# Seven Strassen pairs in place of five in each output projection, with part of the rests on GpSimd

## The chip, the cores and the metric

The kernel runs on one core of a Trainium2 chip. The metric is the time of one execution on the device in microseconds (us); of several runs the median counts. The engines are TensorE (PE; PEld is its weight load), VectorE (DVE), ScalarE (ACT), GpSimd (POOL) and SyncE (SP), whose queue issues the loads and stores here.

## The reference

One layer of an encoder on 512 tokens of width 1024, in fp32: a feed-forward block (FFN), a mixer (short convolution beside a two-way mLSTM), and a second FFN. Each block has a norm ahead and a norm behind it. Cut to the FFN, which the change concerns:

```python
def swiglu(x, w_in, w_out):
    gate, up = jnp.split(x @ w_in, 2, axis=-1)
    return (jax.nn.silu(gate) * up) @ w_out

def reference(...):
    h = swiglu(rmsnorm(x, norm_ffn1_pre), w_ffn1_in, w_ffn1_out)
    x = x + 0.5 * rmsnorm(h, norm_ffn1_post)
    ...   # the mixer, then the second FFN in the same form
```

x is 512x1024, w_in 1024x5632, w_out 2816x1024.

## The kernel before

**Splitting.** TensorE works on a 32-bit format of less precision (fp32r). So each fp32 operand is split: ScalarE casts it to a high part (L292), and a subtraction forms what is left of it, the rest or low part (L294, `split`). `split` takes the engine of that subtraction as its last argument; without one it is VectorE. A product of two operands is three matmuls: high x high, high x low, low x high. Only the first four weight tiles of the program (`ON_POOL`, L234) have their rests formed by GpSimd, with 1024 columns each.

**Input stage of an FFN** (`ffn`, L435). The 2816 columns of gate and up are 22 blocks of 128. The first two are multiplied plainly (L453). For each of the other 20, gate and up are one pair of tiles, and their product with the two halves of x is made by Strassen's scheme of seven products (L431, `mm_part`; 12 matmuls of 256 columns each, 84 a pair). `w_pair` (L151) prepares a pair's weights: four sums of 512 columns on VectorE (L158), then the splits of g, s1, g again and u: rests of 1024, 512, 1024 and 1024 columns, the last named `ul`. The results are joined by VectorE reading PSUM (L503, L505, L508, L484) and multiplied (L509). The fourth product of a pair comes after the first products of the next pair and adds to a bank that L508 has to have read.

**Output stage.** The 22 row blocks of w_out are taken in the order of the list `OUT` (L107). Five pairs of blocks (`SEVEN = 5`) are multiplied by the same scheme, the others plainly. A pair has a part a (products 1, 5, 6, 7) and a part b (2, 3, 4), and each product is six matmuls of 512 columns (L564), 42 a pair; a plain block "k" costs 24 (L589), two of them 48. First come parts a of all pairs; then each part b with a plain block behind it; then the last plain blocks. The last five (`TAIL`) are held back and multiplied token block by token block, each followed by its norm. `w_out_a` and `w_out_b` (L186, L209) form the sums of the weights (L191, L214) and split them; `left_a` and `left_b` (L540, L552) do the same with the activations (L531). After part a of the last pair `taken` moves banks to SBUF, because part b uses them again.

**Order.** TensorE's, VectorE's and the other engines' instructions are put in order by the tile scheduler, outside of a few pinned stretches at the start; each engine runs its instructions in that order. Weights come on SP's queue into four tiles of the pool `rawp`; the split weights live in 12 tiles of `wpool`. `mid` (L604) calls `wgates` (L696), which loads the mixer's gate weights and splits them on GpSimd; they are first used by the mixer's first products (L422).

Of the kernel before, what the change touches and what calls it, by code (L numbers as in the profile page):

```python
# [8 lines left out]
F32 = mybir.dt.float32  # L9
# [7 lines left out]
P = 128  # L17
# [3 lines left out]
KD = D // P  # L21
# [5 lines left out]
EPS = 1e-6  # L27
NEG = -1e30
TAIL = 5
SEVEN = 5  # L30
WARM = 20
WARM2 = 4
ON_POOL = (0, 1, 2, 3)
# [4 lines left out]
def encoder_kernel(ctx: ExitStack, tc: tile.TileContext, a: dict, out: bass.AP):  # L38
# [6 lines left out]
    rawp = ctx.enter_context(tc.tile_pool(name="rawp", bufs=4))  # L45
    gbp = ctx.enter_context(tc.tile_pool(name="gbp", bufs=2))
    t4p = ctx.enter_context(tc.tile_pool(name="t4p", bufs=2))
    t2p = ctx.enter_context(tc.tile_pool(name="t2p", bufs=6))
    small = ctx.enter_context(tc.tile_pool(name="small", bufs=4))
    psum = ctx.enter_context(tc.tile_pool(name="psum", bufs=8, space=PSUM))  # L50

# [54 lines left out]

    OUT = [("a", i) for i in range(SEVEN)]  # L107
    for i in range(SEVEN):
        OUT += [("b", i), ("k", 2 * SEVEN + i)]
    OUT += [("k", k) for k in range(3 * SEVEN, NF)]  # L110

    stream = []
    for w_in, w_out in ((w1i, w1o), (w2i, w2o)):
# [37 lines left out]
    def w_pair(g, u):  # L151


        def wt(n):
            return wpool.tile([P, 1024], F32R, tag="w", name=nm(n))

        def add(o, a_, b_, op):
            nc.vector.tensor_tensor(out=o, in0=a_, in1=b_, op=op)  # L158

        c = (slice(0, 512), slice(512, 1024))  # L160
        s1 = t2()
        add(s1, u[:, c[0]], u[:, c[1]], ALU.add)
        add(u[:, c[0]], g[:, c[0]], u[:, c[0]], ALU.subtract)
        gh, gl = wt("whi"), wt("wlo")
        split(gh, gl, g)
        add(g[:, c[0]], s1, g[:, c[0]], ALU.subtract)
        add(g[:, c[1]], g[:, c[1]], g[:, c[0]], ALU.subtract)
        s1w = wt("ws1")
        split(s1w[:, c[0]], s1w[:, c[1]], s1)
        ch_, cl = wt("whi"), wt("wlo")  # L170
        split(ch_, cl, g)
        uh, ul = wt("whi"), wt("wlo")
        split(uh, ul, u)

        def q(h_, l_, a_, b_):
            return tuple(v[:, r].rearrange("p (k f) -> p k f", k=KD // 2) for v, r in ((h_, a_), (l_, b_)))

        return {
            1: q(gh, gl, c[0], c[0]), 2: q(gh, gl, c[1], c[1]), 5: q(s1w, s1w, c[0], c[1]),
            6: q(ch_, cl, c[0], c[0]), 3: q(ch_, cl, c[1], c[1]),  # L180
            7: q(uh, ul, c[0], c[0]), 4: q(uh, ul, c[1], c[1]),
        }
# [3 lines left out]
    def w_out_a(r0, r1):  # L186

        c = (slice(0, 512), slice(512, 1024))

        def sub(o, a_, b_):  # L190
            nc.vector.tensor_tensor(out=o, in0=a_, in1=b_, op=ALU.subtract)  # L191

        def wt(n):
            return wpool.tile([P, 1024], F32R, tag="w", name=nm(n))

        sub(r1[:, c[0]], r0[:, c[1]], r0[:, c[0]])
        sub(r0[:, c[1]], r1[:, c[1]], r0[:, c[1]])
        t = t2()
        sub(t, r1[:, c[1]], r1[:, c[0]])
        kept.append(t)  # L200
        ah, al = wt("whi"), wt("wlo")
        split(ah, al, r0)
        bh, bl = wt("whi"), wt("wlo")
        split(bh[:, c[0]], bl[:, c[0]], r1[:, c[0]])
        split(bh[:, c[1]], bl[:, c[1]], t)
        return {1: (ah[:, c[0]], al[:, c[0]]), 7: (ah[:, c[1]], al[:, c[1]]),
                5: (bh[:, c[0]], bl[:, c[0]]), 6: (bh[:, c[1]], bl[:, c[1]])}

    def w_out_b(r1):  # L209

        c = (slice(0, 512), slice(512, 1024))
        hi, lo, t = (wpool.tile([P, 1024], F32R, tag="w", name=nm(n)) for n in ("whi", "wlo", "wt"))
        split(hi, lo, r1)
        nc.vector.tensor_tensor(out=r1[:, c[0]], in0=r1[:, c[0]], in1=kept.pop(0), op=ALU.subtract)  # L214
        split(t[:, c[0]], t[:, c[1]], r1[:, c[0]])
        return {2: (hi[:, c[0]], lo[:, c[0]]), 3: (hi[:, c[1]], lo[:, c[1]]), 4: (t[:, c[0]], t[:, c[1]])}

    def w_split(n):
# [57 lines left out]
    nc.gpsimd.memset(nhalf, -0.5)  # L276
    warm = const.tile([P, 256], BF16, name="warm")
    nc.gpsimd.memset(warm, 0.0)
    ones = const.tile([1, P], F32, name="ones")
    nc.gpsimd.memset(ones, 1.0)  # L280
    pw = ps()
    first = [ps() for _ in range(4)]
# [8 lines left out]
    def split(hi, lo, src, eng=nc.vector):  # L291
        latest["hi"] = nc.scalar.copy(out=hi, in_=src)  # L292
        pin(latest["hi"])
        latest["lo"] = eng.tensor_tensor(out=lo, in0=src, in1=f32(hi), op=ALU.subtract)  # L294
        pin(latest["lo"])
# [139 lines left out]
    def ffn(xq, between, finish, mid=None, within=None, ahead=(2, 2, 1, 1), late=None):  # L435
# [104 lines left out]
        def left_a(i):  # L540
            a_, b_ = hcol(2 * i), hcol(2 * i + 1)
            hi, lo = halves()
            s1 = t4()[:, 0:256]
            tt(s1, a_[:, early], b_[:, early], ALU.add)
            split(hi[:, 0:256], lo[:, 0:256], a_[:, later])
            tt(a_[:, early], a_[:, later], a_[:, early], ALU.subtract)
            tt(a_[:, later], s1, a_[:, later], ALU.subtract)
            split(hi[:, 256:512], lo[:, 256:512], s1)
            split(hi[:, 512:1024], lo[:, 512:1024], a_)
            return parts(hi, lo, {1: 0, 5: 256, 7: 512, 6: 768})  # L550

        def left_b(i):  # L552
# [42 lines left out]
        for at, (kind, n) in enumerate(OUT):  # L595
            if kind == "k":
# [4 lines left out]
                hT = (hs[:, q, 0:512], hs[:, q + 1, 0:512])  # L601
                split(hT[0], hT[1], hcol(n))
                ks[n] = (hT, w_get(min(2, len(OUT) - 1 - at)))
                if n == 12 and mid:  # L604
                    mid()
                if n < NF - TAIL:
                    for tb in range(NT):
# [86 lines left out]
    wg = {}  # L694

    def wgates():  # L696
        raw = small.tile([P, KD, 16], F32, tag="rawg", name="rawg", bufs=1)
        queued(raw, wm[:, GT:GT + 16].rearrange("(k p) f -> p k f", p=P))
        gt = bigt(F32R).rearrange("p q f -> p (q f)")
        nc.gpsimd.memset(f32(gt[:, 0:2048]), 0.0)  # L700
# [461 lines left out]
```

## Time and profile before

| | |
|---|---|
| median of 3 runs | 918.28 us (918.09 to 918.73) |
| the profiled execution | 915.36 us, its span 913.7 us |
| granted TensorE clock | 0.999 |
| busy: PE, PEld, DVE, ACT, POOL | 99%, 89%, 78%, 49%, 5% of the span |
| PE on the chain that ended last | 93% |
| first FFN: input stage, output stage | 36 to 228 us, 228 to about 345 us |
| second FFN: input stage, output stage | 594 to 799 us, 799 us to the end |

How to read it: the profile is of one execution, so sums are made against its own time. A row of a timeline gives the start and the length of an instruction, the engine, the line, the operation, what it writes and reads, shape and count, and in brackets how long the engine was idle ahead of it and for whom. A row of the groups gives busy time and mean length in ns, then idle time ahead and for whom. Tile names are the program's; `ps` is a PSUM bank, all other tiles are in SBUF.

### The profile page before, as it was taken

What the parts mean: (1) busy time and instruction counts of PE and PEld (TensorE: products, weight loads), DVE (VectorE), ACT (ScalarE), POOL (GpSimd) and SP (SyncE); (2) the same over time, 40 slices, a digit from 0 to 9 for tenths busy, and PEclk for the clock granted to TensorE, in tenths of its full rate; (3) what the DMA queues carried; (4) which work ended last, traced back from release to release, by engine and by line L of the source; (5) the groups of instructions that cost most, each with busy time, mean ns of one, the idle gap of its engine ahead of it and who ended that gap; (6) DMA issues with size and microseconds to landing.
All of it is one profiled execution on the core that took longest, in us unless ns stands there. A gap on an engine that the chain in (4) does not pass through costs nothing.

```text
span 913.7 us, 15022 instructions
## 1 busy us (share of the span) xinstructions
PE 900.1 (99%) x6015; PEld 816.7 (89%) x6015; DVE 716.2 (78%) x1196; ACT 444.6 (49%) x745; POOL 44.7 (5%) x67
## 2 busy tenths in 40 slices
PE   8999999999999999999999999999999999999997
PEld 7999999999877888987888888999999999977885
DVE  6988998888988359498787746889888988999435
ACT  6655555555456235452434335545545545566311
POOL 5000000000002001000011000000000000000000
PEclk9999999999999999999999999999999999999999
DMA  8233443343335614231422602224343432343402
GB/s 256 68 114 116 119 135 97 102 127 96 93 127 149 199 47 116 63 100 47 116 70 70 197 12 66 74 68 118 112 120 93 118 108 87 119 140 110 162 2 91
DMA packets 126257, 96.47 MB, mean 106 GB/s; under 512 B 4182, under 2 KB 114794, under 8 KB 126187
## 3 DMA queue, kind: packets, MB, share of 16 engines
q1 hardware_dynamic: 126186, 95.51, 35.1%
q8 instruction: 47, 0.77, 0.4%
q14 instruction: 24, 0.19, 0.1%
HBM read 93.40 MB, written 2.10 MB: 105 GB/s over the span
## 4 chain that ended last, share of the span: by engine, by line
PE 93%; DVE 4%; ACT 1%; issue 1%; DMA 1%; SPq 0%; POOL 0%; DVEq 0%; POOLq 0%; ACTq 0%
PE ps L431 43%; PE ps L589 13%; PE ps L422 12%; PE ps L564 9%; PE ps L453 5%; PE ps L1119 5%; PE ps L965 2%; DVE big L294 1%; DVE wlo L294 1%; PE ps L343 1%; DVE big L531 1%; PE ps L1035 1%; DMA x<-in_x_dram 1%; PE ps L983 0%; PE ps L391 0%
## 5 line engine op out<-in xcount | busy, mean ns | idle before, releaser
L294 DVE TENSOR_TENSOR wlo<-raw,whi 128x1024 fp32r<-128x1024 f32 x207 | 245.0, 1192 | 58.9 <-ACT whi L292 44.2
L292 ACT CAST whi<-raw 128x1024 fp32r<-128x1024 f32 x211 | 211.8, 1028 | 145.9 <-DVE raw L158 45.0
L431 PE MATMUL ps<-big,whi 128*128 128x256 f32 x1920 | 264.8, 280 | 0.0
L431 PEld LDWEIGHTS ps<-big,whi 128*128 128x128 f32 x1920 | 243.5, 188 | 0.5
L431 PE MATMUL ps<-big,wlo 128*128 128x256 f32 x960 | 150.9, 280 | 0.0
L431 PEld LDWEIGHTS ps<-big,wlo 128*128 128x128 f32 x960 | 129.3, 188 | 0.0
L589 PE MATMUL ps<-whi,big 128*128 128x512 f32 x384 | 121.9, 395 | 0.2 <-ACT whi L292 0.2
L589 PEld LDWEIGHTS ps<-whi,big 128*128 128x128 f32 x384 | 72.0, 188 | 17.4 <-ACT whi L292 0.6
L422 PE MATMUL ps<-big,whi 128*128 128x512 f32 (+1 forms) x384 | 79.8, 358 | 0.2 <-DVE den L1053 0.2
L564 PE MATMUL ps<-whi,big 128*128 128x512 f32 x240 | 75.9, 395 | 2.6 <-ACT big L292 2.6
L589 PE MATMUL ps<-wlo,big 128*128 128x512 f32 x192 | 75.6, 395 | 0.0
L422 PEld LDWEIGHTS ps<-big,whi 128*128 128x128 f32 x384 | 63.5, 188 | 11.2 <-PE ps L1077 0.4
L431 PE MATMUL ps<-big,ws 128*128 128x256 f32 x480 | 65.3, 280 | 0.0
L431 PEld LDWEIGHTS ps<-big,ws 128*128 128x128 f32 x480 | 60.3, 188 | 0.0
L564 PEld LDWEIGHTS ps<-whi,big 128*128 128x128 f32 x240 | 44.7, 188 | 13.4 <-ACT big L292 3.4
L501 ACT COPY t<-ps 128x256 f32<-128x256 f32 x40 | 14.9, 371 | 72.8 <-PE ps L431 72.7
L292 ACT CAST big<-big 128x512 fp32r<-128x512 f32 (+2 forms) x68 | 36.1, 582 | 23.2 <-DVE big L531 10.8
L564 PE MATMUL ps<-wlo,big 128*128 128x512 f32 x120 | 44.9, 393 | 0.0
L589 PEld LDWEIGHTS ps<-wlo,big 128*128 128x128 f32 x192 | 36.1, 188 | 8.4
L422 PE MATMUL ps<-big,wlo 128*128 128x512 f32 (+1 forms) x192 | 41.1, 356 | 0.0
L294 DVE TENSOR_TENSOR big<-big,big 128x512 fp32r<-128x512 f32 (+2 forms) x68 | 40.7, 634 | 0.1
L422 PEld LDWEIGHTS ps<-big,wlo 128*128 128x128 f32 x192 | 32.1, 188 | 5.5
(212 smaller groups left out, 1143.3 us busy)
## 6 DMA issues: line engine op xcount, KB each, us to landing
raw<-in_w_ffn_in_dram SPq DMA_DIRECT2D x88, 512.0 KB, 4.8
raw<-in_w_ffn_out_dram SPq DMA_DIRECT2D x44, 512.0 KB, 5.0
raw<-in_w_mix_in_dram SPq DMA_DIRECT2D x24, 512.0 KB, 4.5
raw<-in_w_mix_out_dram SPq DMA_DIRECT2D x8, 512.0 KB, 3.6
raw<-in_w_ffn_out_dram SPq DMA_DIRECT2D x10, 256.0 KB, 4.0
out_dram<-x SPq DMA_DIRECT2D x8, 256.0 KB, 2.0
x<-in_x_dram SPq DMA_DIRECT2D x4, 256.0 KB, 4.9
x<-in_x_dram SPq DMA_DIRECT2D x2, 512.0 KB
```

Source lines behind the costliest of these rows:

```text
L292: latest["hi"] = nc.scalar.copy(out=hi, in_=src)
L294: latest["lo"] = eng.tensor_tensor(out=lo, in0=src, in1=f32(hi), op=ALU.subtract)
L343: pin(nc.tensor.transpose(out=pt[:, blk(k)], in_=xs[:, blk(4 * b + k)], identity=ident))
L422: nc.tensor.matmul(o, ww[:, k, :], xk(xT, xx, k, sl), start=n == 0, stop=n == 3 * KD - 1)
L431: pin(nc.tensor.matmul(o, ww[:, k, :], x[xx][:, k, :], start=first and n == 0, stop=n == 11, skip_group_check=True))
L453: pin(nc.tensor.matmul(o, ww[:, k, :], xq_hl(xq, (k // 4, th))[xx][:, k % 4, :], start=n == 0, stop=n == 3 * KD - 1))
L501: nc.scalar.copy(a_[:, h1], x[:, h0])
L531: nc.vector.tensor_tensor(out=o, in0=a_, in1=b_, op=op)
L564: nc.tensor.matmul(acc[tb + t][half], left[n][x][:, blk(t)], right[n][y], start=first and x == y == 0, stop=last_ and x == 1, skip_group_c ...
L589: nc.tensor.matmul(acc[tb][half], hT[hh][:, blk(tb)], w[ww][:, blk(half, 512)], start=fresh and hh == ww == 0, stop=k == NF - 1 and hh == ...
L965: nc.tensor.matmul(pv_, xk(xT, xx, k, blk(tb)), ww[:, k % 2, :], start=n == 0, stop=n == 3 * KD - 1)
L1119: nc.tensor.matmul(acc[half], yy[yi][:, k % 4, blk(tb)], wmo[k][wi][:, blk(half, 512)], start=(n == 0 and yi == 0 and wi == 0), stop=(n == ...
```

## The change

Seven pairs instead of five are multiplied by the scheme in each output projection, so that eight plain blocks are left instead of twelve; in `OUT` a plain block now follows only every second part b. Rests move to GpSimd: in `w_pair` the one of `u` (1024 columns, 20 times in each FFN), in `w_out_a` two of 512 columns, in `w_out_b` one of 512, and in `left_a` one of 512 (each seven times in each FFN). Room for the tiles comes from borrowing: `ones` and the gates' raw weights live in tiles of other pools, and `t2p` has one buffer more. `wgates` is called at block 16 in place of block 12. Lines behind the list `OUT` are numbered two higher after the change.

```diff
-SEVEN = 5
+SEVEN = 7
...
-    t2p = ctx.enter_context(tc.tile_pool(name="t2p", bufs=6))
+    t2p = ctx.enter_context(tc.tile_pool(name="t2p", bufs=7))
...
     OUT = [("a", i) for i in range(SEVEN)]
     for i in range(SEVEN):
-        OUT += [("b", i), ("k", 2 * SEVEN + i)]
-    OUT += [("k", k) for k in range(3 * SEVEN, NF)]
+        OUT.append(("b", i))
+        if i % 2:
+            OUT.append(("k", 2 * SEVEN + i // 2))
+    OUT += [("k", k) for k in range(2 * SEVEN + SEVEN // 2, NF)]
...
         uh, ul = wt("whi"), wt("wlo")
-        split(uh, ul, u)
+        split(uh, ul, u, nc.gpsimd)
...
         bh, bl = wt("whi"), wt("wlo")
-        split(bh[:, c[0]], bl[:, c[0]], r1[:, c[0]])
-        split(bh[:, c[1]], bl[:, c[1]], t)
+        split(bh[:, c[0]], bl[:, c[0]], r1[:, c[0]], nc.gpsimd)
+        split(bh[:, c[1]], bl[:, c[1]], t, nc.gpsimd)
...
-        split(t[:, c[0]], t[:, c[1]], r1[:, c[0]])
+        split(t[:, c[0]], t[:, c[1]], r1[:, c[0]], nc.gpsimd)
...
-    ones = const.tile([1, P], F32, name="ones")
+    ones = t2()[0:1, 0:P]
...
             split(hi[:, 256:512], lo[:, 256:512], s1)
-            split(hi[:, 512:1024], lo[:, 512:1024], a_)
+            split(hi[:, 512:1024], lo[:, 512:1024], a_, nc.gpsimd)
...
-                if n == 12 and mid:
+                if n == 2 * SEVEN + 2 and mid:
...
-        raw = small.tile([P, KD, 16], F32, tag="rawg", name="rawg", bufs=1)
+        raw = t4()[:, 0:KD * 16].rearrange("p (k f) -> p k f", k=KD)
```

GpSimd's order at the end of the first weights and in the first FFN, before. `wlo` is a rest of weights, `rs` a norm's factor:

```order
L294 TENSOR_TENSOR wlo_308<-raw_103,whi_307 128x1024
L700 MEMSET big_3463 128x2048
L706 CAST big_3463<-rawg 128x8x4 x4
L707 TENSOR_TENSOR big_3463<-rawg,big_3463 128x8x4 x4
L310 TENSOR_TENSOR rs_3770<-rs_3768,nhalf 128x1
```

After, where the input stage of the first FFN ends and its output stage begins; `wlo_2770` is the last pair's `ul`, `big_3030` and `big_3065` hold the split activations of the first two pairs:

```order
L296 TENSOR_TENSOR wlo_2647<-raw_2628,whi_2646 128x1024
L296 TENSOR_TENSOR wlo_2770<-raw_2751,whi_2769 128x1024
L296 TENSOR_TENSOR wlo_2885<-raw_2874,whi_2884 128x512
L296 TENSOR_TENSOR wlo_2885<-t_386_2878,whi_2884 128x512
L296 TENSOR_TENSOR big_3030<-big_229,big_3030 128x512
L296 TENSOR_TENSOR wlo_2903<-raw_2892,whi_2902 128x512
L296 TENSOR_TENSOR wlo_2903<-t_393_2896,whi_2902 128x512
L296 TENSOR_TENSOR big_3065<-big_229,big_3065 128x512
```

GpSimd had nothing between its fourth weight tile and the gates; now it has 20 rests of 1024, 21 of 512 for the parts a and 7 of 512 for the parts b in each FFN, one behind the other.

VectorE's order at the same place, before: from the last input pair's `ul` on (`wlo_2770`), with the first output pair's sums (L191) and rests between the joins of the input pairs:

```order
L191 TENSOR_TENSOR t_385_2878<-raw_2874 128x512
L294 TENSOR_TENSOR wlo_2770<-raw_2751,whi_2769 128x1024
L508 TENSOR_TENSOR t_381_2777<-ps_2773,t_381_2777 128x256
L294 TENSOR_TENSOR wlo_2881<-raw_2872,whi_2880 128x1024
L191 TENSOR_TENSOR raw_2892<-raw_2890 128x512
L509 TENSOR_TENSOR big_234<-t_381_2777,t_382_2778 128x256
L294 TENSOR_TENSOR big_3030<-big_229,big_3030 128x256
L294 TENSOR_TENSOR wlo_2885<-raw_2874,whi_2884 128x512
L294 TENSOR_TENSOR wlo_2885<-t_385_2878,whi_2884 128x512
L294 TENSOR_TENSOR big_3030<-t_414_3031,big_3030 128x256
```

After; L510 is the join that was L508, here of the last but one input pair:

```order
L193 TENSOR_TENSOR t_386_2878<-raw_2874 128x512
L296 TENSOR_TENSOR wlo_2881<-raw_2872,whi_2880 128x1024
L510 TENSOR_TENSOR t_382_2777<-ps_2773,t_382_2777 128x256
L193 TENSOR_TENSOR raw_2892<-raw_2890 128x512
L511 TENSOR_TENSOR big_234<-t_382_2777,t_383_2778 128x256
L296 TENSOR_TENSOR big_3030<-big_229,big_3030 128x256
L193 TENSOR_TENSOR raw_2890<-raw_2892,raw_2890 128x512
L193 TENSOR_TENSOR t_393_2896<-raw_2892 128x512
L296 TENSOR_TENSOR big_3030<-t_415_3031,big_3030 128x256
```

The rests `wlo_2770` and `wlo_2885` have left VectorE's order, and the sums for the second output pair have moved up into their place.

## The prediction

> **What bounds the kernel now.** I read the page first: the busy times, then the chain that ended last.
>
> ```profile
> PE 900.1 (99%) x6015; PEld 816.7 (89%) x6015; DVE 716.2 (78%) x1196; ACT 444.6 (49%) x745; POOL 44.7 (5%) x67
> PE 93%; DVE 4%; ACT 1%; issue 1%; DMA 1%; SPq 0%; POOL 0%; DVEq 0%; POOLq 0%; ACTq 0%
> ```
>
> TensorE bounds the whole, and GpSimd (POOL) is nearly unused. So fewer matmuls are worth their time, if nothing else becomes late. Next the windows by stage. The columns are the stretch, its length, then the busy time of PE, PEld, DVE, ACT and POOL with their numbers of instructions, the granted clock, and the DMA share.
>
> ```profile
> 36.00:84.00 48.00, 48.00 (x410) 48.00 (x409) 42.40 (x67) 22.23 (x37) 0.00 (x0) 1.00 0.37 107
> 84.00:228.00 144.00, 144.00 (x1226) 144.00 (x1225) 125.29 (x199) 79.22 (x125) 0.00 (x0) 1.00 0.39 111
> 228.00:261.00 33.00, 33.00 (x170) 27.89 (x169) 30.71 (x60) 16.48 (x29) 0.00 (x0) 1.00 0.40 122
> 594.00:642.00 48.00, 48.00 (x410) 48.00 (x410) 42.47 (x69) 25.45 (x41) 0.00 (x0) 1.00 0.32 92
> 799.00:832.00 33.00, 30.84 (x132) 24.31 (x131) 31.88 (x57) 21.33 (x38) 0.00 (x0) 1.00 0.37 115
> 860.00:885.00 25.00, 25.00 (x110) 20.27 (x109) 6.44 (x7) 3.87 (x5) 0.00 (x0) 1.00 0.06 22
> ```
>
> 36 to 228 us is the input stage of the first FFN (594 to 799 of the second), 228 to 261 and 799 to 832 are the products 1, 5, 6, 7 of the output pairs ("part a"). There VectorE (DVE) is busy 30.7 and 31.9 of 33 us: it is as full as TensorE. The timeline of PE shows that it is already late there:
>
> ```profile
> 263.27 0.50 PE L564 MATMUL ps<-whi,big 128*128 128x512 f32 x1 [1.28 <-ACT big L292]
> 818.08 0.50 PE L564 MATMUL ps<-whi,big 128*128 128x512 f32 x1 [1.28 <-ACT big L292]
> 831.71 0.73 PE L564 MATMUL ps<-wt,big 128*128 128x512 f32 x2 [0.88 <-ACT wt L292]
> 832.66 0.50 PE L589 MATMUL ps<-whi,big 128*128 128x512 f32 x1 [0.22 <-ACT whi L292]
> ```
>
> Those are 3.7 us of waits in the stage that the change rebuilds.
>
> **Matmuls removed.** A pair costs 7 products of 6 matmuls, 42, where two plain blocks cost 48. Two more pairs in each of two FFNs remove 4 x 6 = 24 matmuls of 512 columns. The window 860 to 885 holds 110 of them in 25.00 us, 0.227 us each: **-5.5 us**.
>
> **What the rests cost on either engine.** Groups by shape (mean ns of one after the count), one line's view of its shortest, median and longest, and five consecutive VectorE rows, whose starts give the pitch:
>
> ```profile
> L294 DVE TENSOR_TENSOR wlo<-raw,whi 128x1024 fp32r<-128x1024 f32 x197 | 238.4, 1218 | 58.9 <-ACT whi L292 44.2 <-PE ps L589 8.7 <-PE ps L564 3.8
> L294 POOL TENSOR_TENSOR wlo<-raw,whi 128x1024 fp32r<-128x1024 f32 x4 | 9.6, 2402 | 1.4 <-ACT whi L292 1.3
> L707 POOL TENSOR_TENSOR big<-rawg,big x4: 248/732/1232, 286.1 to 288.7; 128x32 fp32r<-128x32 f32 x4
> 246.59 0.68 DVE L294 TENSOR_TENSOR big<-big,big 128x512 fp32r<-128x512 f32 x1
> 247.19 0.68 DVE L191 TENSOR_TENSOR raw<-raw 128x512 f32<-128x512 f32 x1
> 247.79 1.22 DVE L294 TENSOR_TENSOR wlo<-raw,whi 128x1024 fp32r<-128x1024 f32 x1
> 248.93 0.42 DVE L531 TENSOR_TENSOR big<-big 128x256 f32<-128x256 f32 x1
> 249.26 0.68 DVE L294 TENSOR_TENSOR big<-big,big 128x512 fp32r<-128x512 f32 x1
> ```
>
> VectorE: 0.60 us per 512 columns, 1.14 per 1024, 0.33 per 256. GpSimd: 2.40 per 1024. No row has it at 512: half of 2.40 is 1.20, and with the 0.25 that the shortest L707 took as a fixed part it is 0.25 + 2.15/2 = 1.33. I take 1.26, in the middle.
>
> **Do the two engines run side by side?** This decides the sign. In the profile before, the four long GpSimd subtractions ran while VectorE read PSUM, so they tell nothing. Three short meetings do. The first two rows are the first meeting, the third row is the undisturbed length of such a VectorE subtraction; then two rows of the second and the undisturbed length of that GpSimd instruction; then three rows of the third.
>
> ```profile
> 458.25 0.64 POOL L1018 TENSOR_SCALAR_AFFINE_SELECT t<-t 128x512 f32<-128x512 f32 x1 [14.08 <-ACT t L1016]
> 458.47 0.96 DVE L294 TENSOR_TENSOR big<-t,big 128x512 fp32r<-128x512 f32 x1
> L294 DVE TENSOR_TENSOR ws<-t,ws x40: 676/683/687, 24.4 to 770.9; 128x512 fp32r<-128x512 f32 x40
> 472.81 0.74 DVE L890 SCALAR_TENSOR_TENSOR t<-t,vec,t 128x511 f32<-128x511 f32 x1
> 473.17 0.88 POOL L1018 TENSOR_SCALAR_AFFINE_SELECT t<-t 128x512 f32<-128x512 f32 x1 [7.16 <-ACT t L1016]
> L1018 POOL TENSOR_SCALAR_AFFINE_SELECT t<-t x8: 634/636/881, 442.5 to 489.7; 128x512 f32<-128x512 f32 x8
> 283.99 0.21 POOL L706 CAST big<-rawg 128x32 fp32r<-128x32 f32 x1 [12.82 <-DMA rawg<-in_w_mix_in_dram]
> 284.18 1.24 DVE L294 TENSOR_TENSOR wlo<-raw,whi 128x1024 fp32r<-128x1024 f32 x1 [0.26 <-ACT whi L292]
> 284.29 1.21 POOL L706 CAST big<-rawg 128x32 fp32r<-128x32 f32 x1
> ```
>
> A VectorE subtraction with both inputs in SBUF that starts 0.22 us into a GpSimd instruction takes 0.96 instead of 0.68: it ends 0.54 us after GpSimd, so it hardly began before. A GpSimd instruction that starts while such a VectorE instruction runs takes 0.88 instead of 0.64. A cast of 0.21 takes 1.21 and ends at 285.50, as the 1024-wide VectorE row does (285.42). So they take turns, whole instructions long, one each, and both times add. The Trainium skill says the same ("SBUF — State Buffer", section "Who interferes with whom"): VectorE instructions with two SBUF inputs and GpSimd instructions that read SBUF exclude each other for the whole instruction, and those with a PSUM input do not. These traces agree (+0.28, +0.24 and +1.00 us); the section speaks against the change, since a rest moved at 1.14 then costs the shared path 2.40.
>
> **Part a, by turns.** Of the order after I count from VectorE's L510 of the last but one input pair, which can't run before that pair's seventh product is done, to the last rest of the seventh pair. VectorE has 64 instructions with both inputs in SBUF: 18 of 512, 6 of 1024, 40 of 256, or 10.8 + 6.8 + 13.4 = 31.0 us (6 more read PSUM and can lie beside GpSimd). GpSimd has 21 rests of 512: 26.5 us. By turns: 57.5 us. TensorE does in that time 96 matmuls of 256 columns at 0.117 (48.00 us over 410 in the window 36 to 84), 11.2 us, and 157 of 512 at 0.23, 36.1: 47.3 us. So it must wait about **10 us in each FFN**. Bounds: with 1.20 a rest and two rests done ahead of the count, 53.8 against 47.3, 6.5 us; with 1.33 and the PSUM reads in line as well, 61.0, 13.7 us. The waits of now, 3.7 us, are inside this: **-3.7 + 20 us**. Before, the same count has no GpSimd in it.
>
> VectorE also waits outright for GpSimd here: the L533 rows of part b overwrite what GpSimd still reads, and the rows behind them in VectorE's queue are the next pair's rests. GpSimd holds the raw tiles longer, so that the loads behind them on SP's queue start later:
>
> ```profile
> raw<-in_w_ffn_out_dram SPq DMA_DIRECT2D x44, 512.0 KB, 5.0
> ```
>
> With four raw tiles, two pairs, and some 8 us a pair by turns, 5.0 us stays hidden: nothing. Part b has 7 rests on GpSimd (8.8 us) and 37 us of VectorE before 74 us of TensorE: nothing.
>
> **Input stage.** 20 pairs per FFN each move one 1024-wide rest: 1.22 less and 2.40 more on the shared path, +1.18 us a pair of 84 x 0.117 = 9.8 us. From 84 us on VectorE has 18.7 us free for 14.6 pairs (+17.3): it just fits. From 36 to 84 (and 594 to 642) it has 5.6 us free for 4.9 pairs (+5.8), and not each gap can be used. I take **2 us in each FFN**; the bounds are nothing (GpSimd lies beside the PSUM reads) and 5 us (no gap of 5.6 us is usable).
>
> **The rest of the edits.** The ones row and the gate weights move to borrowed tiles, and the gates' casts, from 283.99 on before, come later by some 10 to 25 us. Their first reader is the mixer's first product:
>
> ```profile
> L422 PE MATMUL ps<-big,whi x384: 275/391/498, 353.6 to 518.4; 128*128 128x512 f32 x128, 128*128 128x256 f32 x64
> ```
>
> 65 us lie between: nothing, and what they overran if that cover were gone. A seventh t2 tile costs nothing.
>
> **Sum.** The profiled execution took 915.4 us (span 913.7): 915.4 - 5.5 - 3.7 + 20 + 4 = 930.2. The median of the runs is 918.3, 2.9 above it: **933 us**, slower. With the bounds: 915.4 - 9.2 + 13 + 0 + 2.9 = 922 to 915.4 - 9.2 + 27.4 + 10 + 2.9 = 946.
>
> **The rivals.** *The engines run side by side* (faster). If long subtractions don't take turns as the short meetings did, or fall into VectorE's waits, VectorE needs per pair of part a 3 x 0.60 + 1.14 + 5 x 0.33 = 4.6 us and GpSimd 3 x 1.26 = 3.8, both below TensorE's 24 x 0.23 = 5.5. Then all waits go: 915.4 - 9.2 + 2.9 = 909. For it: VectorE's free tenth in the input stage. Against: three meetings out of three. Chance 0.14.
>
> *The turns cost what the matmuls gave* (about the same): part a waits only 5 us in each FFN, as GpSimd's rests begin well before my count: 915.4 - 9.2 + 10 + 2.9 = 919. Against: VectorE's rows that feed them stand behind L510. Chance 0.05.
>
> *The input stage waits too* (slower still). The last product of a pair needs VectorE's L510 (L508 before), and between the pair's seventh product and it TensorE has 32 matmuls, 3.7 us. A GpSimd rest of 2.40 and VectorE rows of 1.14 and 0.60 in front of L510 make 4.1: 0.4 us late in each of 40 pairs, 17 us: 950. It decides where a rest on GpSimd regularly begins just ahead of L510; in the order its place varies. Chance 0.13.
>
> **How the numbers follow.** The forecast has 0.68, with 922 to 946 as its own range. A measurement tells about 0.2%, 1.8 us, from no change. Faster is the first rival, 0.14; the second gives 0.03 to the same and 0.02 to slower; with the forecast and the third rival slower has 0.83. The range goes from 917 to 951: it leaves out the first rival and a little above the third.
>
> **What would show it.** Right: GpSimd busy near 40 x 2.4 + 56 x 1.26 = 167 us more, or longer as it waits; VectorE's 512 rows in part a with means well above 0.68; PE waits of some 10 us in all for L296 in each part a, few in the input stage. Wrong: 1024-wide VectorE rests still at 1.22 while GpSimd is busy, and part a without waits (the first rival), or PE waits spread over the input pairs (the third). The matmul term is wrong if PE does not have 24 fewer.

## The result, and the profile after

| | before | after |
|---|---|---|
| median of 4 runs | 918.18 us (917.49 to 918.73) | 954.78 us (951.48 to 956.38) |
| ratio after to before | | 1.0394, 95% interval 1.0365 to 1.0423 |
| the profiled execution | 915.4 us, span 913.7 | 954.3 us, span 952.3 |
| granted TensorE clock | 0.999 | 0.981 |

The change makes the kernel slower by 36.6 us, where 14.7 were forecast. The time lies above the range (917 to 951). First the page after, TensorE's busy row and the chain of work that ended last:

```profile
PE 911.2 (96%) x5991; PEld 820.7 (86%) x5991; DVE 766.8 (81%) x1156; ACT 457.3 (48%) x769; POOL 255.9 (27%) x163
PE 71%; DVE 12%; POOL 3%; issue 3%; ACT 2%; DMA 1%; DVEq 0%; POOLq 0%; SPq 0%; ACTq 0%
```

TensorE has 24 instructions fewer (6015 before), and yet it is busy for 11.1 us longer: some of its work ran at a lower clock. VectorE and GpSimd together have taken 15% of the chain, where VectorE had 4% before. The windows by stage, with the same columns as in the prediction (stretch, length, busy time of PE, PEld, DVE, ACT, POOL with their numbers of instructions, granted clock, DMA share, GB/s):

```profile
36.50:84.00 47.50, 45.94 (x375) 45.57 (x374) 44.88 (x63) 22.34 (x36) 11.72 (x4) 0.96 0.41 123
84.00:235.00 151.00, 151.00 (x1286) 151.00 (x1286) 130.79 (x187) 80.53 (x127) 39.69 (x17) 1.00 0.36 107
235.00:289.00 54.00, 47.44 (x193) 36.55 (x192) 51.09 (x65) 22.45 (x39) 38.03 (x20) 0.91 0.31 98
289.00:296.00 7.00, 0.58 (x2) 0.48 (x2) 5.26 (x7) 5.50 (x10) 1.26 (x1) 0.66 0.58 176
806.00:863.00 57.00, 48.20 (x215) 36.78 (x213) 52.84 (x70) 23.48 (x40) 36.80 (x20) 0.97 0.30 96
863.00:870.00 7.00, 0.68 (x2) 0.50 (x2) 5.26 (x7) 5.53 (x10) 1.26 (x1) 0.86 0.60 176
```

The input stage of the first FFN is full from 84 us on (151.00 of 151.00) and loses 1.6 us ahead of that. The loss is in the output stages: the parts a (235 to 289, 806 to 863), and then, in each FFN, a hole of some 7 us in which TensorE does two matmuls. The third number from the end of a row is the clock: 0.91 and 0.66 in the first FFN, where it was 1.00 before.

What TensorE waited for (engine, its tile and line, what released it; then us in all, times, longest):

```profile
PE ps L566 <- ACT big L294: 13.8, 3, 6.4
PE ps L566 <- DVE wlo L296: 5.4, 5, 1.9
PE ps L566 <- DVE t L505: 3.7, 2, 3.1
PE ps L566 <- POOL wlo L296: 2.7, 2, 2.0
PE ps L433 <- DVE t L510: 2.3, 2, 1.6
PE ps L566 <- POOL big L296: 1.5, 1, 1.5
```

The greatest row names neither VectorE nor GpSimd: it is ScalarE's, and 12.7 of its 13.8 us are the two holes. The input pairs' wait is the fifth row, 2.3 us.

**Where the 38.6 us of span are.** From the starts of TensorE's matmuls in the two traces: what a step exceeds 0.230 us (512 columns) or 0.1175 (256) is lost. Where the clock was at half, as much of a step as one more such matmul is put down to the clock, the rest of the excess to waiting.

| us | matmuls | waits, input stages | waits, parts a | waits in the hole behind them | half clock | sum |
|---|---|---|---|---|---|---|
| before | | 0.8 | 5.3, all of the output stages | | 0 | |
| after | 24 fewer | 4.5 | 20.5 | 12.7 | 12.6 | |
| difference | -5.5 | +3.7 | +15.2 | +12.7 | +12.6 | +38.7 |
| forecast | -5.5 | +4 | +16.3 (20 - 3.7) | 0 | 0 | +14.8 |

Three of the five terms came out as forecast within 1.1 us. Two that the forecast had at nothing make 25.3 us.

**The turns of VectorE and GpSimd** are in the groups (mean ns of one after the count) and in one line's view of GpSimd (shortest, median and longest ns, then first and last start):

```profile
L296 DVE TENSOR_TENSOR wlo<-raw,whi 128x1024 fp32r<-128x1024 f32 x157 | 222.8, 1423 | 79.1 <-ACT whi L294 52.9 <-PE ps L566 10.5 <-PE ps L591 9.4
L160 DVE TENSOR_TENSOR t<-raw 128x512 f32<-128x512 f32 x40 | 45.9, 1147 | 1.0 <-DMA raw<-in_w_ffn_in_dram 0.9
```

```profile
L296 POOL TENSOR_TENSOR wlo<-raw,whi x58: 1252/2412/3401, 10.5 to 854.9; 128x1024 fp32r<-128x1024 f32 x44, 128x512 fp32r<-128x512 f32 x14
L296 POOL TENSOR_TENSOR big<-big,big x14: 1284/1777/5018, 235.5 to 849.4; 128x512 fp32r<-128x512 f32 x14
L296 POOL TENSOR_TENSOR wt<-raw,wt x14: 1262/1302/6518, 287.3 to 900.8; 128x512 fp32r<-128x512 f32 x14
```

VectorE's 1024-wide rest went from 1218 to 1423 ns, one of its four weight sums (L160, L158 before) from 684 to 1147. GpSimd's 512-wide rest takes 1.25 to 1.28 us where nothing disturbs it (forecast 1.26), and 5.02 and 6.52 at worst.

**The hole**, in the first FFN, from the timeline of all engines (start, length, engine, line, operation, and in brackets the idle time ahead and what ended it). L216 is the subtraction of a part b on VectorE, `wt` its cast on ScalarE and its rest on GpSimd; L576 and L578 copy the banks of products 1 and 5 out of PSUM:

```profile
285.78 0.69 DVE L216 TENSOR_TENSOR raw<-raw,t 128x512 f32<-128x512 f32 x1
286.58 0.62 ACT L294 CAST wt<-raw 128x512 fp32r<-128x512 f32 x1 [4.04 <-DVE raw L216]
287.11 1.04 ACT L294 CAST whi<-raw 128x1024 fp32r<-128x1024 f32 x1
287.28 1.30 POOL L296 TENSOR_TENSOR wt<-raw,wt 128x512 fp32r<-128x512 f32 x1 [2.62 <-ACT wt L294]
288.24 1.42 DVE L296 TENSOR_TENSOR wlo<-raw,whi 128x1024 fp32r<-128x1024 f32 x1 [1.77 <-ACT whi L294]
289.70 0.69 DVE L216 TENSOR_TENSOR raw<-raw,t 128x512 f32<-128x512 f32 x1
290.50 0.62 ACT L294 CAST wt<-raw 128x512 fp32r<-128x512 f32 x1 [2.35 <-DVE raw L216]
291.97 1.06 ACT L576 COPY big<-ps 128x512 f32<-128x512 f32 x2
294.82 1.47 ACT L294 CAST big<-big 128x512 fp32r<-128x512 f32 x3
295.53 0.79 PE L566 MATMUL ps<-whi,big 128*128 128x512 f32 x1 [6.42 <-ACT big L294]
```

TensorE's last part a product ends at 289.1. What ends its wait is the cast of the activations on ScalarE (294.82), which stands behind the four copies and one weight cast. The copies could run earlier (in a kernel below they start at 287.04), but they in turn stand behind the `wt` cast of the second part b (290.50), which waits for VectorE's second L216 (289.70), which stands behind a rest (288.24) that waits for a cast and for GpSimd. The part b rows come when VectorE and GpSimd have only just finished the rests of the parts a (GpSimd's last one ends at 284.66). The same rows, shifted by 574 us, stand in the second FFN.

### The profile page after: what moved, and what is told of

Read it like the earlier page. It is cut to its first block, busy times and chain, and to the rows that moved or that the text cites. A ratio compares the mean times of both kernels' runs of the same rounds, so it can differ in the third digit from the quotient of the medians.

```text
span 952.3 us, 15297 instructions
## 1 busy us (share of the span) xinstructions
PE 911.2 (96%) x5991; PEld 820.7 (86%) x5991; DVE 766.8 (81%) x1156; ACT 457.3 (48%) x769; POOL 255.9 (27%) x163
## 4 chain that ended last, share of the span: by engine, by line
PE 71%; DVE 12%; POOL 3%; issue 3%; ACT 2%; DMA 1%; DVEq 0%; POOLq 0%; SPq 0%; ACTq 0%
PE ps L433 31%; PE ps L424 12%; PE ps L591 9%; PE ps L566 8%; PE ps L1121 5%; DVE wlo L296 3%; PE ps L967 2%; POOL big L296 2%; DVE big L296 2%; ACT whi L294 1%; DVE raw L193 1%; PE ps L455 1%; DVE raw L160 1%; DVE t L193 1%; POOL wlo L296 1%
## 5 line engine op out<-in xcount | busy, mean ns | idle before, releaser
L294 ACT CAST whi<-raw 128x1024 fp32r<-128x1024 f32 x215 | 215.0, 1022 | 183.5 <-DVE raw L160 78.1
L296 DVE TENSOR_TENSOR wlo<-raw,whi 128x1024 fp32r<-128x1024 f32 x157 | 222.8, 1423 | 79.1 <-ACT whi L294 52.9
L296 POOL TENSOR_TENSOR wlo<-raw,whi 128x1024 fp32r<-128x1024 f32 (+1 forms) x58 | 131.9, 2274 | 321.5 <-ACT whi L294 243.6
L566 PE MATMUL ps<-whi,big 128*128 128x512 f32 x336 | 115.6, 416 | 19.9 <-ACT big L294 13.8
L433 PEld LDWEIGHTS ps<-big,wlo 128*128 128x128 f32 x960 | 130.0, 189 | 0.0
L424 PEld LDWEIGHTS ps<-big,whi 128*128 128x128 f32 x384 | 63.4, 188 | 11.1 <-PE ps L1079 0.4
L312 POOL TENSOR_TENSOR rs<-rs,nhalf 128x1 f32<-128x1 f32 x24 | 13.6, 566 | 158.3 <-DVE rs L308 149.3
L294 ACT CAST big<-big 128x512 fp32r<-128x512 f32 (+2 forms) x76 | 39.3, 567 | 22.2 <-DVE big L533 11.7
L160 DVE TENSOR_TENSOR t<-raw 128x512 f32<-128x512 f32 x40 | 45.9, 1147 | 1.0 <-DMA raw<-in_w_ffn_in_dram 0.9
L296 POOL TENSOR_TENSOR wt<-raw,wt 128x512 fp32r<-128x512 f32 x14 | 33.7, 2408 | 46.4 <-ACT wt L294 46.4
```

The costliest lines, as they stand in the source:

```text
L312: nc.gpsimd.tensor_tensor(out=r[:, 0:w], in0=acc, in1=nhalf[:, 0:w], op=ALU.pow)
L424: nc.tensor.matmul(o, ww[:, k, :], xk(xT, xx, k, sl), start=n == 0, stop=n == 3 * KD - 1)
L433: pin(nc.tensor.matmul(o, ww[:, k, :], x[xx][:, k, :], start=first and n == 0, stop=n == 11, skip_group_check=True))
L566: nc.tensor.matmul(acc[tb + t][half], left[n][x][:, blk(t)], right[n][y], start=first and x == y == 0, stop=last_ and x == 1, skip_group_c ...
```

## The experiments

Twelve more kernels ran. The nine in this table were each compared with the kernel before on the same chip; three small ones, which compute nothing of the reference, ran once each. The last three columns are worked out from the traces as above; in the output stages the waits of the parts a and of the holes are taken together.

| kernel | us | ratio to before, 95% interval | waits, input | waits, output | half clock |
|---|---|---|---|---|---|
| before | 917.5 | | 0.8 | 5.3 | 0 |
| seven pairs, rests on VectorE | 919.04 | 1.0024 (1.0014 to 1.0034) | 0.8 | 10.4 | 1.6 |
| five pairs, rests on GpSimd | 943.31 | 1.0279 (1.0261 to 1.0298) | 4.8 | 20.4 | 6.3 |
| seven pairs, GpSimd's rests as memsets | 907.27 | 0.9887 (0.9872 to 0.9902) | 0.5 | 1.1 | 0 |
| seven, GpSimd in the input stage only | 920.82 | 1.0045 (1.0029 to 1.0061) | 4.8 | 11.2 | 0 |
| seven, GpSimd in the output stage only | 949.68 | 1.0356 (1.0341 to 1.0372) | 0.6 | 34.1 | 8.9 |
| after | 954.78 | 1.0394 (1.0365 to 1.0423) | 4.5 | 33.2 | 12.6 |
| after, copies ahead | 954.30 | 1.0399 (1.0385 to 1.0414) | 4.7 | 38.9 | 5.6 |
| after, part b rests on VectorE | 951.73 | 1.0383 (1.0361 to 1.0404) | 4.8 | 33.9 | 8.6 |
| after, both of these | 941.58 | 1.0268 (1.0249 to 1.0287) | 4.5 | 26.2 | 5.9 |
| six pairs, rests on VectorE | 919.93 | 1.0021 (1.0012 to 1.0030) | 0.8 | 8.3 | 1.6 |

### Seven pairs with all rests on VectorE

```diff
-        split(uh, ul, u, nc.gpsimd)
+        split(uh, ul, u)
...
-        split(bh[:, c[0]], bl[:, c[0]], r1[:, c[0]], nc.gpsimd)
-        split(bh[:, c[1]], bl[:, c[1]], t, nc.gpsimd)
+        split(bh[:, c[0]], bl[:, c[0]], r1[:, c[0]])
+        split(bh[:, c[1]], bl[:, c[1]], t)
...
-        split(t[:, c[0]], t[:, c[1]], r1[:, c[0]], nc.gpsimd)
+        split(t[:, c[0]], t[:, c[1]], r1[:, c[0]])
...
-            split(hi[:, 512:1024], lo[:, 512:1024], a_, nc.gpsimd)
+            split(hi[:, 512:1024], lo[:, 512:1024], a_)
```

> The seven pairs alone: all rests that the change gave to GpSimd are VectorE's again, the rest of the change stays. Theory S (the loss comes from GpSimd and VectorE excluding each other at SBUF, and from the slower TensorE clock behind the long waits): no loss is left; VectorE is over-full in part a by some 0.9 us a pair, so the 5.5 us of the 24 matmuls come in part: 913 to 920 us, waits of TensorE in part a of 1 to 5 us in each FFN, granted clock 1.00. Rival P (seven pairs are themselves too much for the buffers and the order): 930 us or more, with waits near those of the changed kernel.

919.04 us, 1.0024 times before. So the two more pairs alone give nothing: their 24 matmuls (-5.5 us) are taken back by waits in the output stages, 10.4 us in place of 5.3, and 1.6 us of half clock. TensorE's greatest waits for the output stage are

```profile
PE ps L566 <- ACT big L294: 3.5, 2, 1.8
PE ps L566 <- DVE wt L296: 1.5, 2, 1.2
```

The first is the place of the hole: 1.8 us in each FFN here, 6.4 and 6.3 in the changed kernel.

### Five pairs with GpSimd's rests

```diff
-SEVEN = 7
+SEVEN = 5
```

> The rests alone: five pairs as before, but with GpSimd's rests of the change. Theory S: slower than before, 935 to 950 us, as part a has five sevenths of the changed kernel's turns and no matmul is saved; waits of TensorE of 8 to 14 us in each part a, and some us at half clock. Rival P: within 4 us of before, 918 to 922 us.

943.31 us (the plain blocks stand as in the changed kernel, behind every second part b). With five pairs as before the rests on GpSimd cost 25.9 us, with seven (954.78 against 919.04) some 36. The slowdown is that of the move to GpSimd, and it grows with the number of pairs.

### GpSimd kept as busy, but reading nothing

This kernel leaves out the low parts that GpSimd forms after the change (but for the first input pair's): in place of each subtraction stand three memsets of about its length, so that GpSimd only writes.

```diff
+        if eng is nc.gpsimd and sevens[0]:
+            w = lo.shape[-1]
+            for part in (lo, lo, lo[:, 0:w // 2]):
+                latest["lo"] = eng.memset(f32(part), 0.0)
+                pin(latest["lo"])
+            return
```

> The changed kernel, but where GpSimd forms a rest it writes zeros in three memsets of about the same total length (the low parts that GpSimd made are left out of the sum; the first input pair's rest is still formed). GpSimd is as busy and hands over at the same places, but reads nothing of SBUF. Theory S: the loss goes, 907 to 915 us, VectorE's 512-wide rows are back at 0.68 us, part a has waits below 3 us. Rival H (what costs is a second engine in the chain: its length and its semaphores): about as the changed kernel, 940 to 956 us.

907.27 us. The groups of this kernel show the same VectorE rest as above, and a memset of GpSimd:

```profile
L303 DVE TENSOR_TENSOR wlo<-raw,whi 128x1024 fp32r<-128x1024 f32 x157 | 193.6, 1236 | 104.1 <-ACT whi L295 34.6 <-PE ps L440 22.4 <-PE ps L574 18.7
L300 POOL MEMSET wlo<- 128x1024 f32 x78 | 74.5, 956 | 294.1 <-PE ps L440 187.3 <-ACT whi L295 86.2 <-PE ps L462 11.7
```

VectorE's rest is back at 1236 ns, and the time falls by 47.5 us with the same instructions on TensorE. So GpSimd's being busy is not the cause. The kernel takes away two things at once, though: a memset reads nothing of SBUF, and so it also does not wait for ScalarE's cast, as a subtraction does. What speaks for the reading are VectorE's own rows, which a late GpSimd alone would not lengthen: the rest above, and the weight sum, which is at 681 ns here and at 1147 in the changed kernel. The prediction's first rival gave 909 us for engines that lie side by side; this kernel is that case. The Trainium skill ("SBUF — State Buffer", section "Who interferes with whom") says that a GpSimd instruction that only writes SBUF does not collide with VectorE's two SBUF inputs; this trace agrees (1236 ns against 1423).

### GpSimd's rests in one stage only

```diff
-        split(uh, ul, u, nc.gpsimd)
+        split(uh, ul, u)
```

This is the edit of the kernel with GpSimd in the output stage only. The other one keeps this line and takes the four edits of `w_out_a`, `w_out_b` and `left_a` back.

> Seven pairs, with GpSimd's rests in the input stage only (those of the output stage are VectorE's). Theory S: the seven pairs alone plus some 2 us of waits in each input stage, and nothing in part a but the last input pair's rest: 920 to 928 us. If the input stage's rests are what costs most (the third rival of the prediction): 935 us or more.

> Seven pairs, with GpSimd's rests in the output stage only. Theory S: nearly the whole loss, 944 to 953 us, with 13 us or more of waits in each part a and half clock behind the long ones. If the input stage's rests are what costs most: 930 us or less.

The input stage's part is small: 920.82 us, by the ratios 1.9 us more than with all rests on VectorE (with intervals of some 1.5 us on either side), with 4.0 us more of waits in its input stages. The output stage's part is nearly all: 949.68 us, with 34.1 us of waits and 8.9 of half clock. So the rests of the input stage, 40 of 1024 columns, cost by these waits what was forecast (2 us in each FFN), and what went wrong lies in the output stage.

### How a lone GpSimd instruction gets in

Two kernels compute nothing of the reference. In the first, GpSimd subtracts 512 columns beside ten VectorE rows of a chosen kind; in the second, beside eight rows with two SBUF inputs, sixteen times, in ten of them with a one-column memset or copy of VectorE among the rows.

> Nothing of the reference is computed: ten VectorE subtractions of 512 columns with GpSimd rests of 512 beside them, in seven stretches. Theory S with unfair turns (a single waiting GpSimd instruction gets in only at a gap of VectorE or beside a row that reads PSUM): alone 1.25 us; beside ten rows with two SBUF inputs 6 to 7 us, ending behind the last of them; with the seventh row from PSUM some 4.5 to 5.5 us; three in a queue the first late and the others by turns with VectorE rows of 1.5 us; beside ten rows from PSUM 1.25 us; three memsets undisturbed; beside ten rows that wait for each other 1.3 to 2 us. With fair turns, as in the prediction, a single rest takes 1.9 us at most beside any of them. If there is no exclusion, 1.25 us everywhere.

> Nothing of the reference is computed: a single GpSimd rest of 512 columns beside eight VectorE rows with two SBUF inputs, six times with the rows ahead shortened by steps of 32 columns; then with a memset of one column, then with a copy of one column, as VectorE's fourth row. If a waiting GpSimd instruction that misses the first turn is shut out until VectorE does something without a second SBUF input: some of the six take 1.6 us and the others 5 to 6, and with the memset or the copy none takes more than some 3.8 us. If turns are fair all take 1.6 to 1.9 us (the 4.59 us seen in the earlier bench then had another cause).

From the first, GpSimd's rows and three of VectorE's (two lengths of the timeline are of several instructions, x3 and x6):

```profile
11.86 1.58 POOL L36 TENSOR_TENSOR g<-key,x 128x512 f32<-128x512 f32 x1 [1.47 <-DVE key L44]
19.93 3.69 DVE L48 TENSOR_TENSOR o<-x 128x512 f32<-128x512 f32 x6
20.15 4.59 POOL L36 TENSOR_TENSOR g<-key,x 128x512 f32<-128x512 f32 x1 [6.71 <-DVE key L44]
23.55 0.67 DVE L50 TENSOR_TENSOR o<-p,x 128x512 f32<-128x512 f32 x1
24.15 1.15 DVE L48 TENSOR_TENSOR o<-x 128x512 f32<-128x512 f32 x1
27.85 4.92 POOL L36 TENSOR_TENSOR g<-key,x 128x512 f32<-128x512 f32 x3 [3.10 <-DVE key L44]
```

The same instruction, released at the same point of the same rows, took 1.58 us once (it got in behind one VectorE row) and 4.59 us another time: then the row under way and five more of VectorE's went by, until the one that reads PSUM (23.55). Beside ten rows with two SBUF inputs 6 to 7 us were expected, and it was the 1.58. Alone it took 1.26 us, and beside ten rows that read PSUM 1.27. Three in a queue (27.85) alternated with VectorE, one each. The memsets of the first kernel met no VectorE row, since a one-column copy ahead of them was itself shut out, for 5.93 us. In the second kernel all sixteen got in behind one row, with or without a small instruction among the rows:

```profile
L36 POOL TENSOR_TENSOR g<-key,x x16: 1577/1577/1646, 9.2 to 117.7; 128x512 f32<-128x512 f32 x16
```

So one each, as the prediction assumed, was seen for a queue of GpSimd instructions, and a lone one is either let in at once or shut out. What decides between these was not found: the second kernel was to show it, and has no shut-out in it. In the changed kernel a lone rest shut out looks like this, in the parts a:

```profile
256.39 5.02 POOL L296 TENSOR_TENSOR big<-big,big 128x512 fp32r<-128x512 f32 x1 [3.56 <-ACT big L294]
257.19 1.21 DVE L296 TENSOR_TENSOR wlo<-raw,whi 128x1024 fp32r<-128x1024 f32 x1
260.20 0.41 DVE L486 TENSOR_TENSOR big<-ps,t 128x256 f32<-128x256 f32 x1
261.44 1.47 DVE L533 TENSOR_TENSOR big<-big 128x256 f32<-128x256 f32 x1 [0.83 <-POOL big L296]
```

The rest from 256.39 on gets in when VectorE reaches a row that reads PSUM (260.20), and ends 1.21 us later.

### What lowers the clock

A third kernel that computes nothing of the reference: sixteen waits of TensorE, of 1.3 to 5.4 us, between runs of 60 matmuls.

> Nothing of the reference is computed: TensorE runs streams of 60 matmuls of 512 columns (13.8 us), with a wait for VectorE between them that grows from some 1.5 to 6 us, twice. If waits of the length seen in part a halve the clock: none or few of the short waits (up to 1.5 us) and all of those above some 3.5 us are followed by 3.4 us or more at half clock, with those between differing by their place; a half-clock stretch of 3.4 us costs the stream 1.7 us. If half clock in the changed kernel came from something else, the streams run at full clock.

The granted clock steps on a grid of 3.413 us: each stretch at half clock, here and in the changed kernel, is one to three steps of it long, but for the end of the program. Windows cut on that grid (stretch, length, then busy time of PE, PEld, DVE, POOL, and the clock):

```profile
108.06:111.47 3.41, 0.82 (x4) 0.36 (x2) 2.45 (x4) 0.00 (x0) 1.00 0.00 0
111.47:114.88 3.41, 2.83 (x7) 2.25 (x8) 0.49 (x2) 0.00 (x0) 0.50 0.00 0
265.07:268.48 3.41, 1.54 (x7) 0.94 (x5) 1.77 (x3) 0.00 (x0) 1.00 0.00 0
268.48:271.90 3.42, 1.39 (x6) 1.17 (x7) 1.87 (x4) 0.00 (x0) 1.00 0.00 0
271.90:275.31 3.41, 3.41 (x10) 2.64 (x9) 0.00 (x0) 0.00 (x0) 0.50 0.00 0
```

One wait of 3.90 us lies across two windows here. The window with 1.54 us of work is followed by one at full clock, the window with 1.39 by one at half. All sixteen waits agree: a window at full clock with 1.54 us of work or more is followed by full clock, one with 1.39 or less by half clock. So a wait of 2.18 us lowered the clock where it lay in one window, and one of 3.17 us did not where it lay across two. Each window at half clock costs up to 1.7 us, half of its length. The Trainium skill ("TensorE: Matmul & The Clock Gate", Part 1) has the free-running window of 3413 ns and puts the half clock behind at least one idle window. The grid agrees; here the window need not be idle, some 0.4 of it in work does not hold the clock.

### The hole: copies ahead, and the part b rests back

In one kernel the four copies are kept in their place in the program against the casts for the second part b, so that on ScalarE they stand behind the first part b's casts only:

```diff
         split(hi, lo, r1)
+        if len(kept) > SEVEN - 2:
+            tc.keep_in_program_order(latest["hi"])
...
+        if len(kept) > SEVEN - 3:
+            tc.keep_in_program_order(latest["hi"])
...
-                    nc.scalar.copy(e12, o)
+                    tc.keep_in_program_order(nc.scalar.copy(e12, o))
...
-                    nc.scalar.copy(e22, o)
+                    tc.keep_in_program_order(nc.scalar.copy(e22, o))
```

> The changed kernel, with one thing moved in ScalarE's order: behind the parts a the four copies that free PSUM banks (L576, L578) no longer stand behind the casts for the second and third parts b, which wait for VectorE's and GpSimd's rows of the first; only the casts of the first part b stay ahead. In the changed kernel TensorE waits 6.4 us there in each FFN (up to 295.5 and 869.5 us), followed by two stretches of half clock in the first and two in the second. Theory Q (that wait is the queue on ScalarE, apart from the turns of VectorE and GpSimd): the wait falls to 2 to 3 us in each FFN, a little of it comes back where the second part b's weights are now later, at most one half-clock stretch stays at each place, and the time falls from 955 to 936 to 946 us. Rival T (the wait is the rest of the turns of part a, and the copies would be late in any order): 950 to 957 us, and the wait stays over 5 us. In both, the other waits of the output stages stay at 8 to 12 us in each FFN.

954.30 us: no gain, although the wait at the copies is gone (0.65 us in the first FFN, with the first part b's cast at 286.52 where it was at 286.58). In its place stands one for GpSimd. First two rows of the waits of TensorE, then a row each of VectorE, GpSimd and TensorE from the timeline of this kernel, then the second and third part b's rests in the changed kernel:

```profile
PE ps L570 <- POOL wt L300: 9.1, 2, 5.0
PE ps L570 <- ACT big L298: 1.8, 2, 1.1
```

```profile
296.41 0.68 DVE L218 TENSOR_TENSOR raw<-raw,t 128x512 f32<-128x512 f32 x1
297.88 6.62 POOL L300 TENSOR_TENSOR wt<-raw,wt 128x512 fp32r<-128x512 f32 x1 [9.36 <-ACT wt L298]
304.56 1.65 PE L570 MATMUL ps<-wt,big 128*128 128x512 f32 x3 [4.09 <-POOL wt L300]
```

```profile
291.20 1.26 POOL L296 TENSOR_TENSOR wt<-raw,wt 128x512 fp32r<-128x512 f32 x1 [2.61 <-ACT wt L294]
300.54 6.52 POOL L296 TENSOR_TENSOR wt<-raw,wt 128x512 fp32r<-128x512 f32 x1 [8.08 <-ACT wt L294]
```

The second part b's rest on GpSimd is shut out for 5.4 us by VectorE's rows, and its product waits 4.1 us; in the second FFN it takes 7.56 us, and the product waits 5.0. In the changed kernel this rest was not shut out: it ran inside the hole, from 291.20 on, in 1.26 us. Only the third part b's took 6.52 us, and TensorE did not wait for it. It is the edit that made the second one late: the subtraction that it needs (L218, L216 in the changed kernel) went from 289.70 to 296.41, and the rest fell among VectorE's back-to-back rows. The expectation allowed for a little of this; it took back all that the copies had given (half clock 12.6 to 5.6 us, waits in the output stages 33.2 to 38.9). So neither theory was right as written: the queue on ScalarE was the wait, and without the hole another wait came in its place. The next two kernels take the part b rests back to VectorE, with the copies ahead and without:

```diff
-        split(t[:, c[0]], t[:, c[1]], r1[:, c[0]], nc.gpsimd)
+        split(t[:, c[0]], t[:, c[1]], r1[:, c[0]])
```

> The kernel with ScalarE's four copies moved ahead, and besides the rest of each part b (512 columns, seven in each FFN) back on VectorE; the rests of the input stage and of the parts a stay on GpSimd. With the copies ahead alone, TensorE's wait at the copies fell from 6.4 to 0.6 us in the first FFN, but it then waited 4.1 and 5.0 us for GpSimd's second part b rest, which took 6.62 us (297.88 to 304.50 us) behind VectorE's back-to-back rows, where such a rest takes 1.25 alone. Theory D (two waits stand behind one another, the queue on ScalarE and the lone rest of GpSimd that VectorE's rows shut out; each hides the other): with both gone the waits between the parts a and the first plain block are 0.5 to 3 us in each FFN, no half-clock stretch stays there or one, and the time is 934 to 944 us. Rival T (VectorE is late there from the turns of part a in any case): it stays at 948 to 957 us, with a wait of 5 us or more there for VectorE's rows.

> The changed kernel with the rest of each part b back on VectorE and nothing else; ScalarE's copies stay behind the casts for the second and third parts b. Theory D: the wait at the copies stays (4.5 to 6.5 us in each FFN), as it lies ahead of what the shut-out rest would delay, with its half-clock stretches; 949 to 956 us. If the lone rest of GpSimd alone makes the wait in the changed kernel: 934 to 944 us.

With both, 941.58 us, 13.2 less than the changed kernel; with the part b rest alone, 951.73. The hole's waits, in the first FFN of the kernel with both:

```profile
PE ps L570 <- ACT wt L298: 1.1, 1, 1.1
PE ps L570 <- ACT big L298: 0.3, 1, 0.3
```

and the row for both FFNs of the one with the part b rest alone:

```profile
PE ps L566 <- ACT big L294: 13.0, 3, 6.2
```

Alone, the part b rests leave the hole as it was; alone, the copies trade it for a wait on a part b rest; together they give 13 us. The 0.5 and 3 us of the edits alone are not clear of noise (by the ratios a loss of 0.5 and a gain of 1 us, with intervals of 1.3 us and more on either side). Of the 13, the waits gave 7 and the half clock 6.7: at the place of the holes TensorE's waits fell from 12.7 to 2.9 us, and those ahead came out some 3 us longer.

### Six pairs

`SEVEN = 6` in the kernel with all rests on VectorE.

> Six pairs in each output projection, nine plain blocks less one in place of twelve, all rests on VectorE, as seven pairs with all rests on VectorE took 1.0024 times the kernel before. Matmuls: 12 fewer than before, -2.7 us. If VectorE, already full in the parts a of five pairs, makes TensorE wait in proportion to the pairs (seven pairs: 10.4 us of waits in the output stages instead of 5.3), six pairs wait some 2.5 us more than five: 917 to 919 us, ratio 0.998 to 1.001. If the waits of seven pairs come mostly from the change from parts a to parts b and not from the number of pairs: 914 to 916 us.

919.93 us, 1.0021 times before: between five pairs and seven there is nothing to gain. It has 8.3 us of waits in the output stages, between 5.3 and 10.4, roughly as waits in proportion to the pairs would have it (the time is 0.9 us above the 917 to 919 expected for that). No version here that computes the whole is faster than the kernel before.

## Why the prediction was wrong

**Matmuls removed: right.** 24 fewer, -5.5 us; the other terms add up with it to the measured span.

**The engines take turns: right, and shown.** In the first small kernel three GpSimd subtractions in a queue alternated with VectorE's rows, and without GpSimd's reads the time is 907.27 us. The price of a 512-wide rest, which no row of before had, was 1.25 to 1.28 us against 1.26 forecast.

**Part a by turns: right.** The stretch that the prediction counted, from L510 of the last but one input pair (228.98) to the end of the last rest (284.66), took 55.7 us against 57.5, and in 55.4 of them VectorE or GpSimd had an instruction under way. The waits in the parts a were 8.7 and 11.8 us against 10 each. Lone rests were at times shut out for 2 to 5 us, which the prediction's turns of one each did not have; the stretch came out no longer than the count, presumably because VectorE got on with its own rows meanwhile.

**Input stage: right in its waits.** 1.95 and 1.7 us more of them, against 2 in each FFN; one window at half clock (72.78 to 76.19) made it some 1.5 us dearer. The third rival, waits in each of 40 pairs, was not seen (2.3 us in all for L510).

**"Part b has 7 rests on GpSimd (8.8 us) and 37 us of VectorE before 74 us of TensorE: nothing": this step failed.** It compared sums over the whole part, where the start of the part decided. There a chain of ScalarE, VectorE and GpSimd stood ahead of the copies and of the activations' cast, and TensorE waited 6.4 and 6.3 us, 12.7 us in all. What is late next was asked of VectorE and GpSimd, not of ScalarE's queue. The place in that queue decided: with the copies ahead the wait fell to 0.65 us in the first FFN, although the first part b's cast came at the same time. That place is a product of the order after the change, too: with seven pairs and all rests on VectorE the copies (from 272.59 us on) stand ahead of the first part b's cast (275.37), and the wait is 1.8 us.

**The sum kept the clock: the second failure.** It priced waits as waits alone. They came bunched, and where they took more than half of a 3.413 us window, the next one ran at half clock: 12.6 us more, about half of it in the parts a and most of the rest behind the holes. The prediction's trace showed no half clock in the stages concerned, as its longest wait there was 1.28 us.

With these two terms, 930.2 + 12.7 + 12.6 less the 1.4 us by which the other terms were over their size, the sum gives 954.1 against 954.3 of the profiled execution. That is no independent proof, as the terms are read from the same trace; the evidence that the hole and its half clock were there to be had is the 13.2 us that came back when it was removed without a GpSimd rest taking its place. The half clock's part of the loss in the parts a was not taken out by an experiment of its own.

Still open is why a lone GpSimd subtraction is let in at once in one place and shut out in another; in the small kernels its release came 0.22 us after the start of a VectorE row in both cases.

One sum of the prediction is off without bearing on the outcome: the second rival's 919 us leaves out the 4 us of the input stage, with which it is 923.

## What to carry to other kernels

Before an elementwise instruction with SBUF inputs is moved from VectorE to GpSimd, add both engines' times in the stage with the least slack, as they take turns; and ask of each product at the start of the next stage which queue its last input comes through, as a sum over the stage says nothing about its first microseconds. Price waits of TensorE by how they are bunched: here some 2 us within a window of 3.4 cost up to 1.7 more in clock. Where taking one wait away gives nothing, look for the one that came in its place, and for what the edit itself made late, before the first is called harmless.

## What the runs showed of the hardware that was not expected

- A GpSimd subtraction of 512 columns (1.26 us alone) that is alone in its queue can be shut out by back-to-back VectorE rows with two SBUF inputs for as long as these last: 4.59, 5.02, 6.52, 6.62 and 7.56 us were seen. In the first two it got in at a VectorE row that reads PSUM, in the next two at a pause of VectorE. With three of them in GpSimd's queue the engines alternated (1.58, 1.71 and 1.71 us; seen once).
- The granted clock fell to half for a window of 3.413 us when the window ahead of it, at full clock, held no more than about 1.4 to 1.5 us of matmuls of 512 columns. In the changed kernel the windows on either side of that limit had 1.52 (half) and 1.88 us (full). Busy time is not the whole rule: a window with matmuls of 256 columns had 1.85 and was followed by half, and windows already at half clock had 2.00, 2.35 and 2.53 and were followed by half again.
- GpSimd memsets of the same total length, which only write SBUF, left VectorE's rest at 1236 ns, where reading ones made it 1423.
